# Rotary swaps issued from ScalarE's queue, and weights asked for eight half pieces ahead

## The chip, the cores and the metric

One Trainium2 chip, one core. The metric is the device time of one execution in microseconds (us). Before: 774.34 us, the median of three runs (773.42 to 774.81). Engines are named as in the profile: PE is TensorE, PEld its weight loads, DVE VectorE, ACT ScalarE, POOL GpSimd, SP SyncE; a name with q (SPq) is that engine's instruction queue, which also issues DMAs.

## What is computed

One decoder block on 512 tokens of 1024 channels in float32. Two attention mixers share one projection of the normalised input; the first sums three dilated windows, the second attends to the 128 keys that an indexer selects.

```
h = rmsnorm(x, norm_mix);  proj = h @ w_in
qa, ka, va, qb, kb, vb, qi, ki, wi, ga, gb = split(proj)
qa, ka, qb, kb, qi, ki = rope(each)           # rotary positions
y_a = dilated_mixture(qa, ka, va)             # 8 heads of 64
y_b = indexed_sparse_attention(qb, kb, vb, qi, ki, wi)   # 8 heads, one shared key
merged = sigmoid(ga) * (y_a @ w_up_a) + sigmoid(gb) * (y_b @ w_up_b)
x = x + merged @ w_out
h = rmsnorm(x, norm_ffn)
x = x + (silu(h @ w_gate) * (h @ w_up)) @ w_down
out = rmsnorm(x, norm_final)
```

The rotation of a head's 64 channels is z1 cos - z2 sin and z2 cos + z1 sin, with z1 and z2 the two halves of 32.

## The kernel before

Every matmul is made of three (`mm3`, lines 200 to 203): each operand is split into a rounded part hi and a remainder lo, and hi·hi, lo·hi and hi·lo are added in PSUM.

**Weights.** A `Chunk` (line 132) is a block of columns of a weight, usually 256 columns over the eight blocks of 128 rows. It comes in pieces of 512 columns of storage: one load from HBM into a `raw` buffer (line 153, from SP's queue; 5 buffers), one cast on ACT to `whi` (line 172; 8 buffers), one subtraction to `wlo` (line 164; 8 buffers; on POOL in the attention stage). `more` makes one half of a piece: either load and cast, or the subtraction. So a chunk of eight row blocks is four pieces, eight half pieces, and eight buffers hold two such chunks. Asking for `W[k]` makes all that is still missing up to there. `ahead` (line 189) makes one half piece of the first unfinished chunk of a list, `coming`.

**The queue of parts.** The attention stage (about 80 to 330 us) mixes two streams. `attn_step` (line 719) runs the attention of both halves of a head pair in a pipeline: scores (PE), minimum and scaling (DVE), exponential (ACT), reciprocal (DVE), normalise (POOL), transpose (PE), eviction to hi and lo (ACT, DVE), product with the values (PE). Between the steps `fill` takes parts from `queue`: each is two to four row blocks of a projection (rotary queries and keys, values, gates, up-projections). `run_part` (line 345) runs one. In the kernel before it calls `ahead` only if `MAN[0]` is true, which it never is here, since `DV` is 0 (line 78); so `ahead` runs just eight times (`LEAD`) before the stage begins, and every later chunk is made when its first matmul asks. The queue holds, in order: query and key pair 1; pair 2 with gate chunk 0; pair 3 with gate chunk 1; the shared key and value; values 1; sparse queries with gate chunk 2; the rest of the sparse queries; then gates 3 to 7 and the up-projections.

**The top-k search** of the indexer (line 624) is about 110 DVE instructions, given to the scheduler at the lowest priority once the scores are there; its masks are needed by the sparse heads, which come after the four dilated pairs.

**The order of the work.** PE's order from line 838 on is the order of the program. The other four engines are ordered at build time by a list scheduler: of the instructions that are ready by its own estimate it takes the one of highest priority, attention first (level 2), then parts (level 3), then top-k (level 4), and within a level by place in the program. On the chip each engine runs its list in that order.

**The rotary tiles** (`rope_T`, line 485). A projected tile of 128 rows (two heads, channels on the rows) is copied from PSUM by ACT into `raw` (line 488; two buffers, another tag than the weights'). The 32-row halves of each head are exchanged by DMAs from `raw` into `sw`, 32 rows of 2 KB each (line 491; four for a full tile, two for the one of the shared key). DVE multiplies `raw` by cosines (line 495), `sw` by signed sines (line 498) and adds the two (line 499); then the queries or keys are split for the matmuls (lines 420 to 462). There are 13 such tiles: two of pair 0 before the attention stage, six of pairs 1 to 3, one of the shared key, four of the sparse queries.

Of the kernel before, what the change touches and what calls it, by code (L numbers as in the profile page):

```python
# [38 lines left out]
def hybrid_block(ctx: ExitStack, tc: tile.TileContext, x, norm_mix, w_in, w_up_a, w_up_b, w_out,  # L39
                 norm_ffn, w_gate, w_up, w_down, norm_final, c_rope, c_ropeT, c_mask, out):  # L40
    nc = tc.nc
# [25 lines left out]
    def k2(dt=F32, name="k2"):  # L67
        return kp.tile([P, 512], dt, tag="k2", bufs=K2, name=name)
# [61 lines left out]
    MAN = [False]  # L130
# [58 lines left out]
    def ahead():  # L189

        while coming and coming[0].done():
            coming.pop(0)
        if coming:
            coming[0].more()
# [135 lines left out]
    def defer(n, fn):  # L330

        if MAN[0]:
            later.append([n, fn])
        else:
            fn()

    def settle(n=1):
        for _ in range(n):
            for e in later:
                e[0] -= 1  # L340
            while any(e[0] <= 0 for e in later):
                i = next(i for i, e in enumerate(later) if e[0] <= 0)
                later.pop(i)[1]()

    def run_part():
        cost, part = queue.pop(0)
        part()
        settle()
        if MAN[0]:
            ahead()  # L350
        topk_some(TK[2])
        debt[0] -= cost

    def fill(us):

        debt[0] += us
        with level(3):
            while queue and debt[0] > 0:
                run_part()
        if not queue:  # L360
            debt[0] = min(debt[0], 0.0)

    def drain(until=0):
        with level(3):
            while len(queue) > until:
                run_part()
            if not queue:
                settle(9)
        debt[0] = 0.0
# [115 lines left out]
    def rope_T(p_, rows, then):  # L485

        raw, sw, z = kp.tile([P, 512], F32, tag="rp", bufs=2, name="raw"), k2(name="sw"), k2(name="z")
        nc.scalar.activation(raw, p_, AF.Copy)
        for i in range(rows // 32):
            o = 32 * (i ^ 1)  # L490
            nc.sync.dma_start(sw[32 * i:32 * i + 32, :], raw[o:o + 32, :])
        r = slice(0, rows)

        def straight():
            (nc.vector if RT1 else nc.gpsimd).tensor_tensor(z[r, :], raw[r, :], ropeT[r, 0, :], op=ALU.mult)

        def crossed():
            (nc.vector if RT2 else nc.gpsimd).tensor_tensor(sw[r, :], sw[r, :], ropeT[r, 1, :], op=ALU.mult)
            (nc.vector if RT3 else nc.gpsimd).tensor_tensor(z[r, :], z[r, :], sw[r, :], op=ALU.add)
            defer(1, lambda: then(z))  # L500
        defer(1, straight)
        defer(3, crossed)
        return raw
# [22 lines left out]
    def mqa_parts(res):  # L526

        ws = [stream(win, [(QB + 256 * c, 256)]) for c in range(2)] + [stream(win, [(KB, 128)], per=4)]

        def done_q(i, p_):  # L530
            rope_T(p_, P, lambda z: res.__setitem__(1 + i, queries(z, f"qB{i}")))

        def done_kv(p_):
            kv.append(rope_T(p_, HD, lambda z: res.__setitem__(0, key_twice(z, "kB"))))

        def turn_v():
            t_ = acc("vT")
            for b in range(NB):
                nc.tensor.transpose(t_[:, b * HD:(b + 1) * HD], kv[0][HALF[1], b * P:(b + 1) * P], ident[HALF[1], HALF[1]])
            v = vb()  # L540
            for b in range(NB):
                src = t_[:, b * HD:(b + 1) * HD]
                nc.scalar.activation(v[:, b, 0:64], src, AF.Copy, scale=rs1[:, b:b + 1])
                nc.vector.scalar_tensor_tensor(v[:, b, 64:128], src, rs1[:, b:b + 1],
                                               v[:, b, 0:64].bitcast(F32), op0=ALU.mult, op1=ALU.subtract)
        kv = []
        return ([slot_parts(ws[2], 0, done_kv)] +
                [slot_parts(ws[i // 2], i % 2, lambda p_, i=i: done_q(i, p_)) for i in range(4)], [(0.43, turn_v)], ws)
# [3 lines left out]
    def va_parts(c):  # L552

        get_w = stream(win, [(VA + 256 * c, 256)])

        def done(p_, b):
            for pr in (2 * c, 2 * c + 1):
                if b == 0:
                    va[pr] = ap.tile([P, NB, 2, P], F32R, tag="va", bufs=VAB, name=f"va{pr}")
                src = p_[:, pr % 2 * P:(pr % 2 + 1) * P].rearrange("p (s d) -> p s d", s=2)  # L560
                vh, vl = va[pr][:, b, :, 0:64], va[pr][:, b, :, 64:128]
                nc.scalar.activation(vh, src, AF.Copy, scale=rs1[:, b:b + 1])
                defer(1, lambda vl=vl, src=src, vh=vh: nc.vector.scalar_tensor_tensor(  # L563
                    vl, src, rs1[:, b:b + 1], vh.bitcast(F32), op0=ALU.mult, op1=ALU.subtract))
        return [proj_parts(get_w, 256, b, lambda p_, b=b: done(p_, b)) for b in range(NB)], get_w
# [3 lines left out]
    def qka_parts(pr):  # L569
        get_w = stream(win, [(QA + P * pr, P), (KA + P * pr, P)])  # L570
        qkA[pr] = {}

        def done(m, p_):
            rope_T(p_, P, lambda z: qkA[pr].__setitem__(m, (keys if m else queries)(z, f"qk{m}A{pr}")))
        return [slot_parts(get_w, m, lambda p_, m=m: done(m, p_)) for m in range(2)], get_w

    def gate_parts(base, c, store):

        get_w = stream(win, [(base + c * 256, 256)])

        def part(m, k0, p_):
            if k0 == 0:
                p_.append(acc("gate"))
            W = get_w()
            for k in range(k0, k0 + 2):
                l = (W[k][0][:, m * P:(m + 1) * P], W[k][1][:, m * P:(m + 1) * P])
                mm3(p_[0], l, hT[k], k == 0, k == KT - 1)
            if k0 + 2 == KT:
                t = k2(name="gate")
                nc.vector.tensor_tensor(t, p_[0], rb1[0], op=ALU.mult)  # L590
                defer(1, lambda: nc.scalar.activation(t, t, AF.Tanh, scale=0.5))
                store.append(t)
        res = []
        for m in range(2):
            p_ = []
            res.append([(6 * 512 / 2400, lambda m=m, k0=k0, p_=p_: part(m, k0, p_)) for k0 in range(0, KT, 2)])
        return res, get_w

    def flat(*lists):
        return [x for l in lists for x in l]  # L600
# [51 lines left out]
    def topk_some(n):  # L652
        with level(TKL):
            for _ in range(n):
                if topk and next(topk[0], None) is None:
                    topk.clear()
# [224 lines left out]
    V1, wv1 = va_parts(1)  # L881
    B, TV, (*wq, wkv) = mqa_parts(bT)
    G, wg_ = zip(*[gate_parts(base, c, store) for base, store in ((GA, mA), (GB, mB)) for c in range(4)])
# [1 line left out]
    for i, at in enumerate(GAT):  # L885
        seq[at] = seq[at] + flat(*G[i])
    queue += flat(*seq)
    order = [c() for c in (w1, w2, w3, wkv, wv1, *wq, *wg_)]
    for g in G[len(GAT):]:
        queue += flat(*g)  # L890
    yS = []
# [159 lines left out]
    for b in range(NB):  # L1051
        v = None
        for h in range(2):
            for f in range(NF - LAST, NF):
                mm3(po[b, h], (actT[f][0][:, b * P:(b + 1) * P], actT[f][1][:, b * P:(b + 1) * P]), W[f, h], False, f == NF - 1)
            o = x1[b][h]
# [53 lines left out]
```

## Time and profile before

| | |
|---|---|
| median of three runs | 774.34 us |
| the profiled execution | 774.55 us |
| its span, first to last instruction | 772.8 us |
| PE / DVE / ACT / POOL busy, share of the span | 96% / 56% / 46% / 36% |
| mean granted clock of PE, share of full speed | 0.993 |
| swap DMAs | 50, of 64 KB each |

A busy time is the union of an engine's instructions; issuing a DMA, waiting for a semaphore and branching are the queue's and are not counted as busy. A wait is put down to the instruction that ended it last. In a timeline row the first number is the start, the second the length of a run of like instructions, and a bracket holds the idle time before it and what ended that.

### The profile page before, as it was taken

What the parts mean: (1) busy time and instruction counts of PE and PEld (TensorE: products, weight loads), DVE (VectorE), ACT (ScalarE), POOL (GpSimd) and SP (SyncE); (2) the same over time, 40 slices, a digit from 0 to 9 for tenths busy, and PEclk for the clock granted to TensorE, in tenths of its full rate; (3) what the DMA queues carried; (4) which work ended last, traced back from release to release, by engine and by line L of the source; (5) the groups of instructions that cost most, each with busy time, mean ns of one, the idle gap of its engine ahead of it and who ended that gap; (6) DMA issues with size and microseconds to landing.
All of it is one profiled execution on the core that took longest, in us unless ns stands there. A gap on an engine that the chain in (4) does not pass through costs nothing.

```text
span 772.8 us, 10634 instructions
## 1 busy us (share of the span) xinstructions
PE 744.1 (96%) x3621; PEld 625.2 (81%) x3621; DVE 435.6 (56%) x910; ACT 352.6 (46%) x722; POOL 281.4 (36%) x263
## 2 busy tenths in 40 slices
PE   8988998988999999999999999999999999999995
PEld 7977887886888888888887888888888888888884
DVE  5789989997766557765334344344433343222235
ACT  7366566655666667533425333333333333121233
POOL 2653656645545455422121222222222222222223
PEclk9999999999999999999999999999999999999999
DMA  8352433322432221533232332233223333323202
GB/s 278 80 137 54 102 91 88 89 76 69 117 88 70 73 66 55 176 112 107 82 106 59 109 103 88 83 109 109 84 85 105 109 101 90 105 86 109 83 14 109
DMA packets 68502, 74.53 MB, mean 96 GB/s; under 512 B 5392, under 2 KB 55584, under 8 KB 68448
## 3 DMA queue, kind: packets, MB, share of 16 engines
q1 hardware_dynamic: 68448, 73.86, 32.7%
q8 instruction: 28, 0.46, 0.2%
q14 instruction: 26, 0.21, 0.1%
HBM read 68.46 MB, written 2.10 MB: 91 GB/s over the span
## 4 chain that ended last, share of the span: by engine, by line
PE 82%; DVE 10%; ACT 3%; issue 2%; DMA 1%; SPq 0%; POOL 0%; ACTq 0%; DVEq 0%; POOLq 0%
PE o L202 5%; PE u L203 5%; PE o L203 5%; PE u L202 5%; PE u L201 5%; PE o L201 5%; PE g L203 5%; PE g L202 5%; PE g L201 5%; PE gate L201 3%; PE gate L202 3%; PE gate L203 3%; PE x L203 2%; PE x L201 2%; PE x L202 2%
## 5 line engine op out<-in xcount | busy, mean ns | idle before, releaser
L164 POOL TENSOR_TENSOR wlo<-raw,whi 128x512 fp32r<-128x512 f32 (+1 forms) x156 | 206.1, 1331 | 386.6 <-ACT whi L172 376.4
L172 ACT ACTIVATE whi<-raw 128x512 fp32r<-128x512 f32 (+1 forms) x242 | 149.6, 625 | 240.1 <-PE u L203 70.9
L164 DVE TENSOR_TENSOR wlo<-raw,whi 128x512 fp32r<-128x512 f32 x86 | 71.9, 836 | 128.3 <-ACT whi L172 127.8
L201 PE MATMUL g<-h2h,whi 128*128 128x512 f32 x176 | 68.7, 390 | 0.0
L203 PE MATMUL g<-h2l,whi 128*128 128x512 f32 x176 | 68.7, 390 | 0.0
L202 PE MATMUL g<-h2h,wlo 128*128 128x512 f32 x176 | 68.6, 390 | 0.0
L201 PE MATMUL u<-h2h,whi 128*128 128x512 f32 x176 | 68.5, 389 | 0.0
L202 PE MATMUL u<-h2h,wlo 128*128 128x512 f32 x176 | 68.5, 389 | 0.0
L203 PE MATMUL u<-h2l,whi 128*128 128x512 f32 x176 | 68.5, 389 | 0.0
L201 PE MATMUL o<-whi,ah 128*128 128x512 f32 x176 | 68.5, 389 | 0.0
L202 PE MATMUL o<-whi,al 128*128 128x512 f32 x176 | 68.5, 389 | 0.0
L203 PE MATMUL o<-wlo,ah 128*128 128x512 f32 x176 | 68.5, 389 | 0.0
L684 POOL TENSOR_SCALAR sm<-sm,st 128x256 f32<-128x256 f32 (+3 forms) x64 | 40.0, 632 | 62.4 <-DVE st L683 52.1
L201 PE MATMUL gate<-hTh,whi 128*128 128x512 f32 x128 | 51.6, 403 | 0.0
L203 PE MATMUL gate<-hTl,whi 128*128 128x512 f32 x128 | 50.2, 392 | 0.0
L202 PE MATMUL gate<-hTh,wlo 128*128 128x512 f32 x128 | 50.1, 391 | 0.0
L679 ACT ACTIVATE sm<-sm,st 128x256 f32<-128x256 f32 (+3 forms) x64 | 35.6, 557 | 23.3 <-DVE st L678 23.1
L1025 DVE TENSOR_TENSOR u<-u,rb 128x512 f32<-128x512 f32 x22 | 15.2, 692 | 52.4 <-PE u L203 52.4
L201 PE MATMUL slot<-hTh,whi 128*128 128x512 f32 x104 | 41.7, 401 | 1.8 <-DVE va L563 1.1
L201 PE MATMUL proj<-whi,hTh 128*128 128x256 f32 (+1 forms) x128 | 38.4, 301 | 2.8 <-DVE va L563 1.2
L202 PE MATMUL slot<-hTh,wlo 128*128 128x512 f32 x104 | 40.8, 392 | 0.0
L203 PE MATMUL slot<-hTl,whi 128*128 128x512 f32 x104 | 40.7, 391 | 0.0
(268 smaller groups left out, 1627.0 us busy)
## 6 DMA issues: line engine op xcount, KB each, us to landing
raw<-in_w_in SPq DMA_DIRECT2D x54, 256.0 KB, 3.0
raw<-in_w_gate SPq DMA_DIRECT2D x44, 256.0 KB, 2.9
raw<-in_w_up SPq DMA_DIRECT2D x44, 256.0 KB, 2.9
raw<-in_w_down SPq DMA_DIRECT2D x44, 256.0 KB, 2.8
x<-in_x SPq DMA_DIRECT2D x16, 256.0 KB, 4.0
raw<-in_w_in SPq DMA_DIRECT2D x32, 128.0 KB, 2.5
raw<-in_w_out SPq DMA_DIRECT2D x16, 256.0 KB, 2.6
sw<-raw SPq DMA_DIRECT2D x50, 64.0 KB, 2.0
```

Source lines behind the costliest of these rows:

```text
L164: eng.tensor_tensor(lo, raw, hi.bitcast(F32), op=ALU.subtract)
L172: nc.scalar.activation(hi, raw, AF.Copy)
L201: nc.tensor.matmul(o, l[0], r[0], start=start, stop=False)
L202: nc.tensor.matmul(o, l[1], r[0], start=False, stop=False)
L203: nc.tensor.matmul(o, l[0], r[1], start=False, stop=stop)
L679: nc.scalar.activation(sm, sm, AF.Exp, bias=st[:, 0:1], scale=-1.0, accum_out=st[:, 1:2])
L684: nc.gpsimd.tensor_scalar(sm, sm, st[:, 2:3], 1.0, op0=ALU.mult, op1=ALU.mult)
L1025: nc.vector.tensor_tensor(u, p_, rb2, op=ALU.mult)
```

## The change

Swaps are issued from ACT's queue instead of SP's (line 491). `ahead` is called after every part, whatever `MAN[0]`. The list of chunks that `ahead` works off is put in the order in which the parts use them; before, the gates stood behind all others.

```diff
@@ run_part
         cost, part = queue.pop(0)
         part()
         settle()
-        if MAN[0]:
-            ahead()
+        ahead()
         topk_some(TK[2])
@@ rope_T
         nc.scalar.activation(raw, p_, AF.Copy)
         for i in range(rows // 32):
             o = 32 * (i ^ 1)
-            nc.sync.dma_start(sw[32 * i:32 * i + 32, :], raw[o:o + 32, :])
+            nc.scalar.dma_start(sw[32 * i:32 * i + 32, :], raw[o:o + 32, :])
@@ the list of chunks
-    order = [c() for c in (w1, w2, w3, wkv, wv1, *wq, *wg_)]
+    order = [c() for c in (w1, w2, wg_[0], w3, wg_[1], wkv, wv1, wq[0], wg_[2], wq[1], *wg_[3:])]
```

## Rows read from the trace of the kernel before

**Rows 1.** The head of the page: span, and busy time of each engine.
```profile
span 772.8 us, 10634 instructions
...
PE 744.1 (96%) x3621; PEld 625.2 (81%) x3621; DVE 435.6 (56%) x910; ACT 352.6 (46%) x722; POOL 281.4 (36%) x263
```

**Rows 2.** Stages: length, busy us of each engine (instructions), clock, DMA share, GB/s.
```profile
40.00:80.00 40.00, 33.59 (x195) 29.52 (x194) 36.68 (x61) 26.63 (x55) 16.24 (x16) 0.96 0.37 93
80.00:120.00 40.00, 40.00 (x196) 33.66 (x195) 37.44 (x107) 23.59 (x48) 24.31 (x21) 1.00 0.42 106
120.00:192.00 72.00, 63.76 (x346) 53.83 (x345) 67.81 (x175) 43.45 (x102) 43.15 (x39) 0.98 0.30 78
192.00:240.00 48.00, 48.00 (x235) 40.07 (x235) 33.19 (x72) 29.49 (x66) 25.31 (x24) 1.00 0.37 96
240.00:320.00 80.00, 79.21 (x425) 67.39 (x424) 50.92 (x148) 52.63 (x132) 40.29 (x51) 1.00 0.26 78
```

**Rows 3.** PE's waits, 40 to 80 us: total us, times, longest.
```profile
PE dots L613 <- ACT relu L861: 3.8, 3, 1.8
```

**Rows 4.** PE's waits, 82 to 320 us.
```profile
PE pT L693 <- POOL sm L684: 1.9, 3, 1.5
PE pT L693 <- DVE ptl L698: 1.5, 3, 0.8
...
PE y L710 <- DVE ptl L698: 0.3, 1, 0.3
```

**Rows 5.** The swap tile sw: ns min/median/max, first and last us, waits, landing.
```profile
L491 SPq DMA_DIRECT2D sw<-raw x50: 507/582/1610, 50.3 to 225.7; - x50
...
  DMA sw<-raw: 3.7, 2
...
DMA to landing us min/median/max: 1.9/2.0/3.3
```

**Rows 6.** SP's own waits over the whole span.
```profile
SPq L153 <- POOL wlo L164: 475.3, 142, 14.7
```

**Rows 7.** SP's timeline, 94 to 116 us.
```profile
96.59 2.41 SPq L491 DMA_DIRECT2D sw<-raw  x4
102.58 6.64 SPq L153 DMA_DIRECT2D raw<-in_w_in  x3
109.33 3.00 SPq L491 DMA_DIRECT2D sw<-raw  x4
```

**Rows 8.** ACT's timeline behind four rotary copies, and one copy (L488).
```profile
50.35 1.09 ACT L861 ACTIVATE relu<-dots 128x512 f32<-128x512 f32 x2
...
62.29 0.87 ACT L861 ACTIVATE relu<-dots 128x384 f32<-128x384 f32 x2
...
99.47 0.60 ACT L488 ACTIVATE raw<-slot 128x512 f32<-128x512 f32 x1 [0.24 <-ACT qk0A L422]
...
113.68 0.37 ACT L697 ACTIVATE pth<-pT 128x256 fp32r<-128x256 f32 x1
...
133.03 0.61 ACT L679 ACTIVATE sm<-sm,st 128x384 f32<-128x384 f32 x1
```

**Rows 9.** Tiles named raw, 44 to 230 us: ns min/median/max, first and last.
```profile
L164 POOL TENSOR_TENSOR wlo<-raw,whi x48: 1265/1310/1828, 43.2 to 224.3; 128x512 fp32r<-128x512 f32 x48
...
L488 ACT ACTIVATE raw<-slot x13: 574/597/600, 49.7 to 221.4; 128x512 f32<-128x512 f32 x13
```

**Rows 10.** DVE's waits, 80 to 240 us.
```profile
DVE ptl L698 <- ACT pth L697: 3.8, 4, 2.4
```

**Rows 11.** ACT's waits, 44 to 205 us.
```profile
ACT va L562 <- DVE va L563: 11.0, 5, 4.0
ACT qk0A L422 <- DVE z L499: 9.7, 4, 2.7
```

**Rows 12.** ACT's timeline: a weight cast in the gate stage.
```profile
249.81 0.63 ACT L172 ACTIVATE whi<-raw 128x512 fp32r<-128x512 f32 x1 [0.50 <-PE gate L203]
```

**Rows 13.** DVE's groups by line, 80 to 185 us: busy us, mean ns, idle before.
```profile
L629 DVE MAX8 top<-cur 128x8 f32<-128x256 f32 (+2 forms) x43 | 21.9, 541 | 0.0
```

## The prediction

> **What bounds the kernel now.** I read the page's head first: of a span of 772.8 us TensorE (PE) is busy for 744.1, so all that any reordering can win is in PE's idle time [rows 1]. The profiled execution took 774.55 us, 1.75 more than its span and 0.2 above the median of 774.34; the sums below are differences, and I add them to the median.
>
> Second, the table by stages tells where that idle time is [rows 2]. PE lacks 6.4 us of 40 in the stage 40 to 80 us and 8.2 us of 72 in the stage 120 to 192 us; it lacks nothing from 80 to 120 and from 192 to 240, and 0.8 us from 240 to 320. The change touches only what is issued from about 50 us (first swap) to about 320 us (last queued weight chunk). So 15 us is the ceiling of a gain, were every stall there to vanish. In the same rows VectorE (DVE) is busy for 37.4 of 40 and 67.8 of 72 us, while ScalarE (ACT) is busy for 23.6 of 40 and 43.5 of 72, that is 60%: ACT has room on the average, DVE has next to none.
>
> Third, who holds PE. From 40 to 80 us it is mainly ACT's relu eviction [rows 3]; from 82 to 320 us its eight waits name POOL's normalise and DVE's softmax, low halves and evictions, and no row names a weight tile, whi, wlo or a DMA [rows 4]. So neither the swaps nor the weights are what PE waits for directly. A swap can reach it only through DVE, or through what ACT does late.
>
> **Part 1: the swaps leave SP's queue.** There are 50 swap DMAs in 13 rope tiles (twelve of four, one of two), each 0.582 us of issue on the queue that issues it, 2.0 us from issue to landing [rows 5]. Removing them frees 50 x 0.582 = 29.1 us of SP. What is that worth? SP waits 475 us of the span for POOL to free a raw weight buffer [rows 6], so its own time is covered many times over: 0 us. If the cover were gone, SP's 29.1 us would move weight loads, and these have the lead told in part 3.
>
> The swaps themselves could come sooner, because some stand in line behind a weight load that waits for POOL. The worst case is the tile copied at 99.47 us: three weight loads stand ahead of its swaps, and the first is issued at 109.33, some 9 us after the copy ended [rows 7, 8]. But all that DVE ever idles for a swap is 3.7 us in 2 waits [rows 5], and PE's list has no wait for a rotated query or key [rows 4]. I take 0 us, with a gain of up to 3.7 us as the bound.
>
> **Part 2: the same 50 issues stand in ACT's queue.** No row shows a DMA issued by ACT, so the cost needs bounds. An issue takes 0.582 us on SP [rows 5]; the nearest row for ACT is this one. Each issue holds the instructions behind it, and since the swap reads what the copy just wrote, ACT cannot issue the first before that copy is done. Four in a row hold ACT for 4 x 0.6 = 2.4 us, as the 2.41 us row of SP shows at an undisturbed tile, and 3.00 us where one is slow [rows 7].
>
> What is queued behind? I went through ACT's timeline around each of the 13 copies [rows 9]. Behind four of them stands work that another engine already waits for: behind the first two, relu evictions (at 50.35 and 62.29 us), on which PE's score matmuls wait [rows 3, 8]; behind the sixth, the pT eviction at 113.68, for which DVE idles 2.4 us already [rows 8, 10]; behind the seventh, the softmax exponentials at 133.03 [rows 8]. In five others before 190 us ACT afterwards stands idle for DVE; its longest single waits of that kind are 2.7 and 4.0 us, 20.7 us over nine waits [rows 11], as long as a block of swaps, so I cost these at 0. If that cover went, each would cost up to 2.4. The last four copies end with the one at 221.4 us [rows 9] and lie nearly all in the stage where PE is never idle and ACT is busy 29.5 of 48 us [rows 2]: 0 again, with the same price per copy if the cover fails.
>
> The price of each of the four lies between 0.6 us (the scheduler, which orders all engines but PE, threads one issue between two evictions) and 2.4 us (all four stand together). I take the middle, 1.5 us, since nothing in these rows speaks for either end: 4 x 1.5 = **6.0 us**.
>
> **A rule against the gain, and one for the cost.** The Trainium skill, "DMA: Bandwidth & Descriptors", section "Issuing engines are not separate DMA queues", says that DMAs from any engine run on the same 16 DMA engines, and that spreading them only saves sequencer time, usually small. Here the trace agrees that there is nothing to save (SP's 475 us of waiting); taken at "usually small" for ACT too, the sum would be 0, which is the third rival below. "Perfetto Trace Analysis", section "DMA Instruction — HWDGE (DVE, Sync)", has the sequencer held until the descriptors are written, and the descriptor generator locked by one user at a time; by it ACT would pay the full issue, and more where a weight load is being issued. No run here shows it for ACT.
>
> **Part 3: weights asked for eight half pieces ahead.** The number of casts, subtractions and loads is the same; only their place in the program, and so their priority on ACT, POOL and SP, moves forward. One chunk is eight half pieces (four casts, four subtractions), and the eight whi buffers hold two chunks. The trace shows that this lead is already there: in the gate stage the cast at 249.81 us waits for PE to release a buffer, not for its data [rows 12], while PE is still in the chunk before the one whose pieces already lie ready. The data are ahead as far as the buffers go, so asking earlier cannot bring them earlier: 0 us. The new order of the list only makes those calls ask for the chunk that is used next. Bounds: the earlier place may put a weight subtraction of 1.3 us [rows 9] ahead of POOL's normalise, for which PE waits 1.9 us in 3 waits today [rows 4], or take one away. I keep 2 us to either side for it.
>
> **Sum.** 0 (SP) + 0 (swaps earlier) + 6.0 (ACT) + 0 (weights) = 6.0 us; 774.3 + 6.0 = **780.3 us**.
>
> **The rivals.**
> First, ACT's late work cascades through DVE. DVE is nearly full from 80 to 192 us [rows 2], and it runs its instructions in a fixed order, so a wait for ACT there is lost, and PE meets it later. Then not four but seven or more of the nine copies before 190 us pay their whole block: 7 x 2.4 = 17 us, 791 us; all nine, 8 x 2.4 + 1.2 = 20.4, 795 us. It decides where exponentials and pT evictions stand behind the swaps. For it: DVE's 94% share of that stage [rows 2]. Against it: ACT's waits for DVE, which swallow delays [rows 11].
>
> Second, on the other side, the new order frees DVE's queue. The order on ACT, DVE and POOL is laid out anew when swaps no longer wait behind weight loads. PE's waits from 120 to 192 us are for DVE's results, and much of DVE's work there is the top-k search (its maxima alone 21.9 us up to 185 us [rows 13]), which PE needs only for the heads of the sparse attention, after all heads of the dilated one; with the softmax and the evictions half as late PE gets back half of 8.2 us, 4.1 us: 770.2 us. It decides if the rotated tiles, now landing up to 9 us sooner, leave DVE's queue before the softmax steps that stand behind them. For it: the swap that comes 9 us late today [rows 7, 8]. Against: DVE's 3.7 us in all, and ACT's 29.1 us of new work.
>
> Third, nothing that can be measured: the issues fall where ACT idles (some 40% of the stages from 80 us on [rows 2]), or they are short on ACT, and the weight calls change nothing because the buffers already set the pace. That is 774.3, with 1 to 1.5 us to either side.
>
> **How the numbers follow.** A measurement of this kernel tells 0.2%, about 1.5 us, from no change; the runs of before spread over 1.4 us. Forecast (4 to 10 us more): 0.42. Cascade: 0.14. DVE's queue freed: 0.28. Nothing: 0.16. So slower 0.56, no change 0.16, faster 0.28. The range reaches from 770 (the second rival's 4.1 us) to 791 (seven full blocks); the forecast's own range is 777 to 785 (four copies at 0.6 to 2.4 us, with some of the weights' bound).
>
> **What the changed profile should show.** Step by step: the swap rows on ACT's queue, x50, near 0.58 us each; SP without them and its waits for POOL no smaller; blocks near 2.4 us between a copy and ACT's next activation. PE's waits for ACT (relu, pT, the exponentials through POOL) should grow in the stages 40 to 80 and 120 to 192, and PE idle there should rise by about 6 us, with none in 192 to 240. Casts should still wait for PE's buffers, and no wait of PE should name a weight. The forecast is wrong if a swap takes ACT well under 0.3 us, if the swaps stand apart from the copies in time that ACT idles anyway, or if PE's idle time from 120 to 192 falls.

## The result and the profile after the change

The changed kernel takes 783.38 us (median of 4 runs, 782.47 to 784.40), the kernel before on the same chip 773.88 (773.18 to 774.81): ratio 1.0122, 95% interval 1.0103 to 1.0141, or 9.5 us more. 780.3 was forecast, with a range of 770 to 791. Behind line 349 the changed kernel's lines are one lower: its L490 is L491 of before.

The head of the page of the changed kernel, the counterpart of [rows 1]; TensorE (PE), VectorE (DVE), ScalarE (ACT) and GpSimd (POOL) run as many instructions as before:

```profile
span 782.6 us, 10604 instructions
...
PE 750.0 (96%) x3621; PEld 630.5 (81%) x3621; DVE 441.6 (56%) x910; ACT 351.2 (45%) x722; POOL 281.5 (36%) x263
```

The same five stages as in [rows 2], for the changed kernel (length, busy us of PE, PEld, DVE, ACT and POOL, granted clock, DMA share, GB/s):

```profile
40.00:80.00 40.00, 34.97 (x212) 30.74 (x211) 35.30 (x53) 25.62 (x52) 16.88 (x15) 1.00 0.36 93
80.00:120.00 40.00, 37.26 (x171) 30.94 (x171) 38.60 (x102) 21.83 (x46) 22.17 (x19) 0.96 0.34 86
120.00:192.00 72.00, 60.25 (x317) 51.46 (x316) 69.32 (x168) 41.75 (x95) 40.20 (x35) 0.93 0.30 75
192.00:240.00 48.00, 48.00 (x243) 40.23 (x242) 32.57 (x78) 28.00 (x67) 26.77 (x27) 1.00 0.41 105
240.00:320.00 80.00, 79.28 (x419) 67.27 (x417) 49.93 (x142) 53.33 (x131) 41.44 (x48) 1.00 0.23 67
```

PE's idle time falls by 1.4 us in the first stage, rises from 0 to 2.7 in the second and from 8.2 to 11.8 in the third: 20.2 us in all five, against 15.4. The clock is part of the loss too: 0.96 for 1.00 over 40 us and 0.93 for 0.98 over 72, less a gain of 0.04 over the first 40, is some 3.6 us (1.6 + 3.6 - 1.6). And the first swap is issued at 52.8 us instead of 50.3 [rows 5], though nothing ahead of it was changed; the experiments with the swaps alone and with the weights alone have 50.5 and 50.1. So some 2.3 us of this profiled run are its own start. The sum of the three, an estimate of 10.7, stands against 9.8 us of longer span; it is rough because the edges of the stages now cut the work elsewhere.

What PE waits for in the changed kernel, 44 to 330 us (total us, times, longest), the counterpart of [rows 3, 4]:

```profile
PE slot L201 <- DVE va L562: 5.8, 2, 3.0
PE gate L201 <- DVE gate L589: 3.3, 1, 3.3
PE dots L612 <- ACT relu L860: 2.5, 4, 1.1
PE proj L201 <- DVE gate L589: 2.5, 1, 2.5
...
PE proj L201 <- DVE va L562: 1.5, 1, 1.5
```

The same operations in the kernel before, in the same window:

```profile
PE proj L201 <- DVE va L563: 1.2, 2, 0.9
...
PE slot L201 <- DVE va L563: 1.1, 1, 1.1
PE slot L201 <- DVE gate L590: 0.8, 1, 0.8
```

This is the surprise of the profile. The waits that grew are not for ACT, which got 50 more things to do, but for two evictions by DVE, which has the same 910 instructions as before: 13.1 us for va and gate (5.8 + 3.3 + 2.5 + 1.5), where the kernel before has 3.1 (1.2 + 1.1 + 0.8). The wait for relu, which was to grow, fell from 3.8 [rows 3] to 2.5.

DVE's timeline in front of the longest wait for a gate, then PE's row that ends the wait:

```profile
133.28 1.47 DVE L628 MAX8 top<-cur 128x8 f32<-128x512 f32 x3
...
134.73 0.68 DVE L633 MATCH_REPLACE8 cur<-top,cur 128x512 f32<-128x512 f32 x1
...
136.24 0.68 DVE L628 MAX8 top<-cur 128x8 f32<-128x512 f32 x1
136.84 0.54 DVE L677 CUSTOM_DVE_ANT_0 sm<-sc,lc 128x384 f32<-128x384 f32 x1
...
141.34 1.26 DVE L589 TENSOR_TENSOR gate<-gate,rb 128x512 f32<-128x512 f32 x2
```

```profile
142.06 0.50 PE L201 MATMUL gate<-hTh,whi 128*128 128x512 f32 x1 [3.27 <-DVE gate L589]
```

Top-k work (MAX8 and MATCH_REPLACE8) fills DVE from 132.9 to 136.8 us. The softmax row stands behind it, and ten more operations later the eviction that PE wants. In three short stretches around that wait the clock column shows what idleness costs afterwards:

```profile
138.00:142.00 4.00, 0.79 (x4) 0.32 (x2) 4.00 (x11) 3.89 (x11) 2.66 (x4) 1.00 0.00 0
142.00:146.00 4.00, 3.94 (x15) 3.38 (x16) 4.00 (x12) 2.90 (x5) 1.27 (x1) 0.70 0.10 20
146.00:150.00 4.00, 4.00 (x17) 3.16 (x16) 4.00 (x16) 3.00 (x9) 1.24 (x3) 0.88 0.22 49
```

PE is busy for 0.79 of 4 us, and then runs 4 us at 0.70 and 4 at 0.88 of its clock: 0.30 x 4 + 0.12 x 4 = 1.7 us behind an idleness of some 3.3.

The swap tile of the changed kernel (ns min/median/max, first and last; then DVE's idle time for it), beside [rows 5], and the waits of SyncE's (SP's) queue, beside [rows 6]:

```profile
L490 ACTq DMA_DIRECT2D sw<-raw x50: 514/602/1746, 52.8 to 237.4; - x50
...
  DMA sw<-raw: 1.7, 2
```

```profile
SPq L153 <- POOL wlo L164: 541.2, 148, 16.8
```

The swaps are on ACT's queue, 0.602 us each. SP gained only waiting time, 541 us for 475.

### The profile page after: what moved, and what is told of

Read it like the earlier page. It is cut to its first block, busy times and chain, and to the rows that moved or that the text cites. A ratio compares the mean times of both kernels' runs of the same rounds, so it can differ in the third digit from the quotient of the medians.

```text
span 782.6 us, 10604 instructions
## 1 busy us (share of the span) xinstructions
PE 750.0 (96%) x3621; PEld 630.5 (81%) x3621; DVE 441.6 (56%) x910; ACT 351.2 (45%) x722; POOL 281.5 (36%) x263
## 3 DMA queue, kind: packets, MB, share of 16 engines
q1 hardware_dynamic: 66048, 70.58, 30.6%
## 4 chain that ended last, share of the span: by engine, by line
PE 81%; DVE 11%; issue 3%; POOL 2%; ACT 1%; DMA 1%; SPq 0%; POOLq 0%; DVEq 0%; ACTq 0%
PE o L202 5%; PE o L201 5%; PE u L202 5%; PE u L203 5%; PE u L201 5%; PE o L203 5%; PE g L203 5%; PE g L202 5%; PE g L201 5%; PE gate L201 3%; PE gate L202 3%; PE gate L203 3%; PE sc L612 2%; PE x L203 2%; PE x L202 2%
## 5 line engine op out<-in xcount | busy, mean ns | idle before, releaser
L164 POOL TENSOR_TENSOR wlo<-raw,whi 128x512 fp32r<-128x512 f32 (+1 forms) x156 | 208.9, 1350 | 374.4 <-ACT whi L172 373.2
L683 POOL TENSOR_SCALAR sm<-sm,st 128x256 f32<-128x256 f32 (+3 forms) x64 | 37.7, 596 | 86.9 <-DVE st L682 75.6
L202 PE MATMUL gate<-hTh,wlo 128*128 128x512 f32 x128 | 50.3, 393 | 0.0
```

Source lines behind the costliest of these rows:

```text
L164: eng.tensor_tensor(lo, raw, hi.bitcast(F32), op=ALU.subtract)
L202: nc.tensor.matmul(o, l[1], r[0], start=False, stop=False)
L683: nc.gpsimd.tensor_scalar(sm, sm, st[:, 2:3], 1.0, op0=ALU.mult, op1=ALU.mult)
```

## The experiments

Two theories were put up. **H**: the issues hold ACT, and work behind four copies comes late, as forecast. **L**: the compiler's scheduler, which orders all engines but PE, lays the others out anew once the swaps are on ACT, and that layout is what loses. The kernel before was run beside each group. Its medians are 774.58 us (one half at a time, order of the program), 776.07 (issues or layout alone, moved top-k), 775.01 (the two even spreads) and 775.93 (twice as many issues, the shorter spread); "over before" is always against these, by the ratio of the runs and not by the difference of the medians.

### One half of the change at a time

The first has the swaps alone, the second the weight calls and their list alone:

```diff
-            nc.sync.dma_start(sw[32 * i:32 * i + 32, :], raw[o:o + 32, :])
+            nc.scalar.dma_start(sw[32 * i:32 * i + 32, :], raw[o:o + 32, :])
```

> The swaps on ACT's queue alone, the calls of ahead and the list as before. If the whole loss comes from the swaps (both theories below), this takes what the changed kernel takes, 782 to 785 us; if the weights asked ahead carry part of it, 776 to 780.

```diff
-        if MAN[0]:
+        if True:
             ahead()
...
-    order = [c() for c in (w1, w2, w3, wkv, wv1, *wq, *wg_)]
+    order = [c() for c in (w1, w2, wg_[0], w3, wg_[1], wkv, wv1, wq[0], wg_[2], wq[1], *wg_[3:])]
```

> The calls of ahead and the new list alone, the swaps on SP's queue. My step says 0: 773 to 775.5 us, PE's idle time in each stage within 0.5 us of the kernel before. If asking earlier puts subtractions ahead of POOL's normalise, 776 or more, with longer waits of PE for POOL.

Measured: swaps alone 782.29 us, ratio 1.0095 (1.0078 to 1.0113), 7.4 us over before. Weights alone 775.06, 1.0008 (0.9994 to 1.0023): nothing. A stage and SP's wait of the second, the same as in [rows 2, 6]:

```profile
120.00:192.00 72.00, 63.83 (x351) 53.61 (x350) 67.69 (x174) 43.49 (x102) 43.14 (x39) 1.00 0.31 78
```

```profile
SPq L153 <- POOL wlo L164: 473.9, 142, 14.9
```

The loss is that of the swaps. The traces also tell the order in which each engine ran its instructions. In the swaps-alone kernel PE runs its 3621 matmuls in the order of before. DVE has another instruction than before in 252 of its 910 places, all of them between 66 and 245 us, ACT in 169 of 722 and POOL in 33 of 263.

One word in the source, and DVE, which issues none of these transfers, has another order. With the weight part alone no engine's order changes. The changed kernel runs in the order of the swaps-alone kernel on all four engines.

### The order taken from the program, with and without the issues

In both the attention stage runs on every engine in the order in which the program was written, so that moving the swaps moves few compute instructions and none far (in the traces 29 of DVE by up to 6 places, 40 of ACT by up to 12); both have the weight calls and their list, and the second has the swaps on ACT as well.

```diff
-    DV = 0
+    DV = 1
```

> Swaps on SP; in the attention stage PE, DVE, ACT and POOL all run in the order of the program instead of the scheduler's. It is the base of the next run; its own time is not forecast closely, 770 to 800 us.

> The same fixed order with the swaps on ACT's queue, each block right behind its copy. Theory H (the issues hold ACT, and the work behind them is late for DVE and PE): 6 to 17 us above the run with the swaps on SP. Theory L (the loss is a new order that the scheduler lays out for DVE, ACT and POOL, top-k instructions ahead of what PE waits for): with the order held the same, 0 to 2 us above it.

Measured: 800.09 us (1.0325, 1.0301 to 1.0349) and 799.81 (1.0338, 1.0296 to 1.0381). This order is 25 us worse than the scheduler's, and in it 50 issues on ACT cost nothing that can be told. That spoke for L, but it is weak: an order with so much waiting may hide an issue that a tighter one can't.

### Issues without the layout, layout without the issues

The decisive pair. Edges without a semaphore chain the instructions of DVE, ACT and POOL in the attention stage as a table of names (PIN) lists them. The first takes the swaps on ACT and the table of the kernel before; the second leaves the swaps on SP and takes the table of the swaps-alone kernel. In the traces PE, DVE, ACT and POOL run their compute instructions in exactly the order of the kernel the table is from, in each of the two.

```diff
+def pin(tc, nc):
+    made = {i.name: i for i in nc.cur_bb.bb.instructions[MARK[0]:]}
+    for names in PIN.values():
+        kept = [made[f"I-{n}"] for n in names if f"I-{n}" in made]
+        for a, b in zip(kept, kept[1:]):
+            if a.engine == b.engine:
+                tc.add_manual_dep(b, a.name, mybir.DependencyInfo(mybir.DependencyClass.NoSync, mybir.DependencyReason.DATA), reason="pin")
...
```

> Swaps issued by ScalarE, but the compute instructions of VectorE, ScalarE and GpSimd pinned to the order that they have in the kernel before (TensorE's is the same in all kernels); old weight list. The 50 issues are all that differs. Theory H (an issue holds ScalarE's queue at four copies that TensorE's next work stands behind): the whole loss shows, 780 to 784 us, ratio 1.007 to 1.012. Theory L (the issues cost nothing by themselves; the loss is the new order in which the scheduler lays out VectorE, ScalarE and GpSimd): 774 to 776 us, ratio 0.998 to 1.003.

> Swaps issued by SP as before, but VectorE, ScalarE and GpSimd pinned to the order that they have in the kernel with the swaps on ScalarE. The order is all that differs from the kernel before. Theory H: 773 to 776 us, ratio 0.998 to 1.003. Theory L: the loss stays without a single issue on ScalarE, 780 to 784 us, ratio 1.007 to 1.012.

Measured: issues alone 780.24 us, ratio 1.0063 (1.0039 to 1.0087), so 4.9 us (3.0 to 6.8). Layout alone, without one issue on ACT, 783.92, ratio 1.0112 (1.0083 to 1.0140), so 8.7 us. By its ratio the first lies between what the two theories expected; the second is where L expected it. Each theory is right of something, and the two losses don't add: together, in the swaps-alone kernel, they are 7.4 and in the changed kernel 9.5 us, no more than the layout by itself within the intervals.

PE's waits with the layout alone, 44 to 330 us, are those of the changed kernel, name by name:

```profile
PE slot L201 <- DVE va L563: 5.8, 2, 3.1
PE gate L201 <- DVE gate L590: 5.1, 1, 5.1
PE proj L201 <- DVE va L563: 2.9, 1, 2.9
PE dots L613 <- ACT relu L861: 2.5, 4, 1.1
PE proj L201 <- DVE gate L590: 2.4, 1, 2.4
```

With the issues alone, in the order of before, they are those of [rows 3, 4], grown: ACT's relu from 3.8 to 4.8, POOL's normalise from 1.9 to 2.5, the low halves from 1.5 to 2.1. All of PE's waits in this window are 18.4 us for 15.5; the rest of the 4.9 us was not traced to a place.

```profile
PE dots L613 <- ACT relu L861: 4.8, 4, 2.4
PE pT L693 <- POOL sm L684: 2.5, 4, 1.1
PE pT L693 <- DVE ptl L698: 2.1, 3, 1.0
```

How an issue gets there is seen at the sixth rope tile of the issues-alone kernel, on ACT's timeline and in PE's row that ends the wait:

```profile
116.10 0.63 ACT L447 ACTIVATE qk1A11l<-qk1A11l 64x512 fp32r<-64x512 f32 x1 [0.74 <-POOL qk1A11l L446]
116.17 2.44 ACTq L491 DMA_DIRECT2D sw<-raw  x4
118.71 0.60 ACT L488 ACTIVATE raw<-slot 128x512 f32<-128x512 f32 x1 [1.97 <-DMA sw<-raw]
...
121.00 0.61 ACT L679 ACTIVATE sm<-sm,st 128x384 f32<-128x384 f32 x1
```

```profile
121.78 0.33 PE L693 MATMUL pT<-ident,sm 128*128 128x128 f32 x1 [1.15 <-POOL sm L684]
```

Before, the same copy (L488) followed the last qk1A11l at once, at 112.55. Now four issues stand between, those of the fifth tile, and the copy, the pT eviction and the exponentials behind it come some 2 us later; PE's transposes then wait 1.15 and 1.00 us for POOL's normalised rows, where they did not wait before. At the seventh tile the issues stand singly between the exponentials, and PE waits for nothing there.

### Twice as many issues

The same pinned order of before with each swap DMA cut in two halves of 256 columns: 100 issues.

```diff
-            nc.scalar.dma_start(sw[32 * i:32 * i + 32, :], raw[o:o + 32, :])
+            [nc.scalar.dma_start(sw[32 * i:32 * i + 32, c:c + 256], raw[o:o + 32, c:c + 256]) for c in (0, 256)]
```

> As the kernel with swaps on ScalarE and the order of the kernel before pinned, but each quarter swap is two transfers of 256 columns, so that ScalarE issues 100 instead of 50. If the 4.9 us of that kernel are the issues' time on ScalarE's queue, the loss about doubles: 9 to 12 us over the kernel before, 783 to 787 us. If it is a fixed thing (other semaphores, another ring, the order of arrival), it stays: 4 to 6 us, 779 to 781 us.

Measured: 806.05 us, ratio 1.0395 (1.0376 to 1.0414), 30.6 us over before: six times the loss, not twice. The same spot on ACT's timeline, then PE's row that ends the wait and the two stretches around it:

```profile
125.38 0.63 ACT L447 ACTIVATE qk1A11l<-qk1A11l 64x512 fp32r<-64x512 f32 x1 [0.95 <-POOL qk1A11l L446]
125.44 5.01 ACTq L491 DMA_DIRECT2D sw<-raw  x8
130.50 0.60 ACT L488 ACTIVATE raw<-slot 128x512 f32<-128x512 f32 x1 [4.49 <-DMA sw<-raw]
```

```profile
133.56 0.48 PE L693 MATMUL pT<-ident,sm 128*128 128x128 f32 x1 [6.39 <-POOL sm L684]
```

```profile
127.00:134.00 7.00, 0.61 (x3) 0.18 (x1) 1.77 (x6) 2.96 (x8) 1.81 (x3) 0.83 0.14 33
134.00:138.00 4.00, 3.58 (x11) 2.96 (x11) 3.96 (x9) 1.26 (x2) 0.40 (x1) 0.50 0.34 82
```

The block grows from 2.44 to 5.01 us, but PE's wait grows from 1.15 to 6.39. From the start of the last qk1A11l to PE's transpose it is 8.18 us for 5.68: 2.5 us more, the longer block. The other 2.7 us were lost ahead of it: with 50 issues ACT starts that instruction 4.5 us before PE runs out of work (at 120.63), with 100 only 1.8 us (at 127.17). So the delays of earlier blocks have eaten the lead that ACT had. Behind the wait PE runs 4 us at the lower of its two clocks (0.50, or 1.2 of 2.4 GHz). The expectation took the price to be proportional, and fell.

Not all of the 30.6 us need be ACT's time: the halves are also twice as many transfers, DVE's idle time for swaps is 7.6 us for 3.0, and no run has 100 issues on SP. What the loss shows is that it isn't proportional.

### Is it where the top-k operations stand?

In the changed layout they run in front of what PE waits for, so they were moved by themselves. The table of DVE alone is edited: the 111 top-k operations stand behind as many other DVE operations as in the other kernel. The lines below, and those of the spreads further on, are the rule that makes the table; the kernels differ in the table itself. First the swaps-alone kernel with the top-k of before, then the kernel before with the top-k of the swaps-alone kernel:

```diff
+# count: for each top-k operation, the other DVE operations ahead of it in the other kernel
+for done, name in enumerate(others):
+    while count and count[0][0] <= done:
+        order.append(count.pop(0)[1])
+    order.append(name)
```

> Swaps on ScalarE and the order of the swaps-on-ScalarE kernel, but VectorE's 111 top-k operations stand behind as many other VectorE operations as in the kernel before. Theory L with the top-k operations as its cause (they run ahead of evictions, the exponentials' input and the softmax row that TensorE waits for): 774 to 777 us. Theory L with the rest of the order as its cause (softmax rows, copies, the rotary work): 780 to 784 us, as the changed kernel. Theory H: 780 to 784 us too.

> Swaps on SP and the order of the kernel before, but the 111 top-k operations stand where the swaps-on-ScalarE kernel has them, by the count of other VectorE operations ahead. Theory L with top-k as its cause: 780 to 784 us. Theory L with the rest of the order: 773 to 777 us. Theory H: 773 to 776 us.

Measured: 787.19 us (1.0142, 1.0106 to 1.0178) and 784.21 (1.0117, 1.0092 to 1.0143). The second says that the places of the top-k alone can cost 9.1 us, with all else as before; the first, slower than either theory expected, that putting them back mends nothing. PE's waits of the second kernel, 44 to 330 us, name yet other operations:

```profile
PE pT L693 <- POOL sm L684: 5.4, 3, 3.7
PE dots L613 <- ACT relu L861: 4.1, 3, 1.8
PE sc L613 <- DVE st L678: 3.6, 3, 1.8
```

Then the top-k was spread evenly, one in two DVE operations, up to the place where the first mask is near (the other operations keep their order, and none of the top-k stands earlier than before; the spread begins at operation 101, in the second kernel at 104), with the swaps on SP and, in the swaps-alone order, on ACT:

```diff
-    place = own[name]
+    place = max(own[name], 101 + (300 - 101) * i / 110)
```

> Swaps on SP, ScalarE and GpSimd in the order of the kernel before; on VectorE the 111 top-k operations stand evenly between the others up to the place where the first mask is near (one in two instead of some in a row), the others in their old order. If VectorE's top-k runs are what TensorE waits behind between 120 and 200 us, TensorE loses up to 8 us less there: 766 to 772 us, and a version faster than both kernels. If the waits come from the chains themselves (copy, subtraction, softmax row), or if VectorE now loses time behind each late operand: 773 to 778 us.

> The same even spread of the top-k operations, with the swaps on ScalarE and the order of the swaps-on-ScalarE kernel in all else. Theory T (that order loses because runs of top-k operations stand ahead of evictions that TensorE waits for): those waits go, and this kernel is within 2 us of the spread kernel with its swaps on SP, or up to 5 above it by the issues alone (measured as 4.9). Theory R (the rest of that order loses): 6 to 12 us above it, 780 us or more.

Measured: 780.41 us (1.0079, 1.0061 to 1.0097) and 789.88 (1.0196, 1.0173 to 1.0218). Theory T of the second fell: with no run of top-k left, PE still waits for va and gate, here between 44 and 330 us:

```profile
PE slot L201 <- DVE va L563: 7.9, 2, 5.3
...
PE gate L201 <- DVE gate L590: 3.9, 1, 3.9
```

The first wasn't faster either: it is slower than both its expectations. Its stages say where it won and lost:

```profile
120.00:192.00 72.00, 65.53 (x358) 55.85 (x357) 62.89 (x173) 44.19 (x102) 41.25 (x38) 0.98 0.31 80
192.00:240.00 48.00, 44.38 (x208) 36.17 (x207) 45.50 (x98) 26.69 (x59) 23.66 (x22) 0.96 0.32 84
```

PE gets 1.8 us back from 120 to 192 (65.53 for 63.76) and loses 3.6 from 192 to 240, where the late top-k now fills DVE to 45.5 of 48 us. So the last experiment ended the spread 45 DVE operations sooner:

```diff
-    place = max(own[name], 101 + (300 - 101) * i / 110)
+    place = max(own[name], 101 + (255 - 101) * i / 110)
```

> As the spread of the top-k operations with the swaps on SP, but ended 45 VectorE operations earlier, so that the last long mask operations do not stand among the softmax rows ahead of the second half. If the spread gains 3 us up to 200 us and only its late end lost 6 (VectorE 45.5 of 48 us busy in 192 to 240): 770 to 774 us, faster than both kernels. If the nearer spacing takes the gain away: 774 to 777 us.

Measured: 778.91 us (1.0042, 1.0026 to 1.0058): the best of the moved orders, but above what was expected of it (770 to 777) and still 3.3 us slower than before. No kernel here beat the one before.

## Why the prediction was right in its number and half right in its reason

**The number.** 6.0 us more were forecast, 9.5 measured: the sign is right, and the time stands in the likeliest case's own range of 777 to 785. That it does is in part luck: another cause, of a like size, took the place of the one that was priced.

**Part 1 was right.** Nothing shows a worth of SP's freed 29.1 us: its wait for POOL grew to 541 us, and no wait of PE from 44 to 330 us names a load. What the earlier swaps gave stayed inside the bound: DVE's idle time for them fell from 3.7 to 1.7 us.

**Part 2 was right as a price, wrong as an account of this kernel.** With the order held still the 50 issues cost 4.9 us (3.0 to 6.8) where the sum said 6.0, through the kind of chain it named: a block of four takes 2.44 us (2.4 forecast), the exponentials come late, POOL's normalise and PE's transposes behind them, and relu in the first stage. The places are only in part those it priced: at the sixth copy the block in the way is that of the fifth tile, which it had at 0, and the seventh tile costs PE no wait. The step that failed is the one under the price: it went through ACT's timeline of before and priced an issue behind each copy as if all else stayed in its place. In the changed kernel it doesn't. The layout is another, it loses 8.7 us without a single issue on ACT, and in it the issues cost nothing more that these runs can tell. So the forecast signs of the profile were wrong: PE's waits for ACT didn't grow (relu 2.5 and a copy 0.8 us, for 3.8), its idle time rose from 80 to 120 us, where no loss was seen coming, and fell from 40 to 80. From 120 to 192 us it did rise, by 3.5 us. And of the thirteen tiles only two have their four issues as one block behind the copy (2.44 and 3.32 us); the others stand in ones and twos.

The part's rule from the Trainium skill, "Perfetto Trace Analysis", section "DMA Instruction — HWDGE (DVE, Sync)", that the sequencer is held until descriptors are written, agrees with the blocks of 2.44 us for four and 5.01 for eight on ACT's queue, as far as their length goes; when descriptors are written no run shows. Its other half, one user of the descriptor generator at a time, would make an issue longer beside one on SP. That isn't seen: in the changed kernel the 11 issues on ACT that overlap a weight load's issue on SP have a median of 0.603 us and a longest of 0.614, the other 39 a median of 0.601.

**Part 3 was right.** The weight calls alone are 1.0008 (0.9994 to 1.0023), SP waits as long as before, and no wait of PE names a weight.

**The rivals.** The second, a new order that frees DVE, had the premise that counts (ACT, DVE and POOL are laid out anew) and the wrong sign. It argued that top-k would move out of the way; in the changed kernel a run of it stands ahead of the gate's eviction, and the experiments that moved it won nothing back. The first, a cascade at 17 to 20 us, didn't come with 50 issues; 100 do what it describes, at 30.6 us, with PE's wait for the normalised rows at the head of its list. The third, nothing, is out by the interval. Its rule, from the Trainium skill, "DMA: Bandwidth & Descriptors", section "Issuing engines are not separate DMA queues", was right that there was nothing to gain. Its "usually small" is said of the time that is saved; of the time that is paid on ACT these runs show 4.9 us for 50 issues and 30.6 for 100.

**What stays open.** Which displaced operation of the new layout costs most isn't settled. Top-k places alone can do it (9.1 us), and aren't the whole of it here. Why the scheduler chose this layout was not looked into; that a kernel pinned to its own order keeps its time wasn't run by itself, though the layout-alone kernel repeats the waits of the changed one, at 783.92 us for 783.38, and the edges leave the number of instructions as it was (10635 for 10634 with the swaps on SP).

## What to carry to other kernels

Where a scheduler orders the engines, moving one DMA to another queue is two changes: the issue on the new queue, and a new order for engines that never see the transfer. Predict them apart, and measure them apart by holding the order still once with and once without the issues. In a stage as full as this one (DVE busy for 67.8 of 72 us), another order of the work that PE doesn't need yet can cost as much as the edit itself: all seven other orders that were tried here lost, 3 to 25 us, two of them run only with the swaps on ACT. And an issue on a compute engine's queue is paid for where the slack behind it ends, so don't take the price to be proportional: here the second dose was dearer than the first.

## What the runs showed that had not been expected

ACT's queue runs ahead of its engine. In the changed kernel a swap is issued at 129.35 us while an exponential works, and the next activation begins before the issue has ended:

```profile
128.94 0.72 ACT L678 ACTIVATE sm<-sm,st 128x512 f32<-128x512 f32 x1
129.35 0.51 ACTq L490 DMA_DIRECT2D sw<-raw  x1
...
129.67 0.49 ACT L678 ACTIVATE sm<-sm,st 128x256 f32<-128x256 f32 x1
```

So a single issue between two activations is nearly free here, while four in a row held ACT for 1.97 of their 2.44 us in the issues-alone kernel: threads of one, which a scheduler can lay, and blocks of four are different prices. And PE's clock makes a wait longer than it looks: by the rows above, 3.3 us of idleness cost an estimated 1.7 us more in the 8 us after it.
